# Dealing independent filler matmuls to the first steps and to the closing iterations of an attention loop, with two query loads moved ahead of it

## The chip, the cores and the metric

One Trainium2 chip, one core of it. The metric is the device time of one execution, in microseconds (us). The kernel before took 986.68 us (median of three runs, 985.72 to 988.01).

## What is computed

One layer of a hybrid encoder, on 1024 prompt rows and 64 sample rows of 1024 channels:

```python
h = rms_norm(x, norm_w) @ w_in          # 6144 columns: q, k, v, z of two branches, two gates
# branch sb: stick-breaking attention, 8 heads of 64
w = exp(log_beta + suffix_sum(log_keep))          # over all earlier keys
# branch cb: softmax attention over a band of chunks, with a relative bias, 8 heads of 64
p = softmax(q.k/8 + bias)
h = sigmoid(g_sb) * ((o_sb * silu(z_sb)) @ w_proj_sb) + sigmoid(g_cb) * ((o_cb * silu(z_cb)) @ w_proj_cb)
y = x + h @ w_out
```

The sample rows attend to 512 cached keys as well. Keys and values are outputs too.

## The kernel before, in words

Everything lies in one function whose Python code writes out the order of every engine's instructions. Each engine works through its own list in that order and waits on semaphores. TensorE multiplies float32 values as three products of rounded parts (`hi*hi`, `hi*lo`, `lo*hi`).

Stages: the input projection (to about 524 us), a lead (524 to 548), the attention loop (548 to 831), a tail (831 to 848), the projection of branch cb (L974) and the output projection (L1488).

**The attention loop** runs over a list `seq` of 136 steps: branch sb, then cb; in each four pairs of heads; in each pair t = 8 (the sample rows, one step for both heads), then t = 0 to 7, two heads each. A step passes through a pipeline over the iterations i of the loop:
- `qk(i)`: the scores, TensorE L1080 into `z`. In sb a sigmoid on ScalarE follows (L1083), in cb a VectorE operation with the bias (L1085).
- in sb `mid` one iteration later: a VectorE scan (L1102) on `be`. In cb `soft` (ScalarE exp, L1093) and then `mid` (VectorE reciprocal L1104, ScalarE scaling L1105).
- `tr(i - 3)`: transposes on TensorE (L1133) into `pt`, which has two PSUM buffers; ScalarE (L1142, L1138) or VectorE (L1144) copies them to `wT`.
- `av` at the next iteration, when two steps of a pair of row blocks are there: TensorE L1172 into `o`; VectorE multiplies it with the gate `zt` (L1181 in sb, L1183 in cb); GpSimd issues the store of `zt` (L745).

At t = 8 or 0 and others `prefetch` issues loads for later steps from the SyncE queue (SP): queries `sq` through `load_q` (four transfers by the helper at L51), keys `ks`, values (L785 to L787), and `zt` (L1150).

**The fill.** A generator `run_fill` holds matmuls that do not depend on the attention. `fill(n)` writes out the next n of them. They are:
- four units of 72 matmuls (L832), each in three pieces of 24 for columns 0 to 383, 384 to 767 and 768 to 1087. Piece 1 of a unit starts with the split of the next weights: ScalarE rounds `wraw` to `whi` (L116), VectorE or GpSimd makes the rest `wlo` (L123). A piece ends with a ScalarE evacuation to `sg` (L807).
- then the projection of branch sb, `proj_sb`: 24 groups of 12 matmuls (L932) on the accumulator `acc`, which has two PSUM buffers. Two groups share a gate tile `gt` (L912, two buffers). VectorE evacuates each group (L936). Of every six groups the last two have 320 columns, the others 384.

The lead takes 6 x 24 = 144 of the matmuls and issues the loads of the first pair between them. The loop deals the third unit (72) over branch sb, in proportion to the width of a step, and 252 plus 12 over branch cb. The fourth unit is held back until the loop's iteration 73: before that `fill` only notes what it owes, and iteration 73 pays it at once:

```python
if prog[0] == len(units) - 2 and "sb" not in late:
    owed[0] = n
    return
```

Four iterations behind the last step (i = 136 to 139) drain the pipeline, with no fill. In the tail, `load_og` loads branch cb's outputs by column piece (L889, into `ot`, two buffers for two pairs of heads each), `make_og` rounds them on ScalarE (L893) and subtracts on GpSimd (even pairs) and VectorE (odd pairs, L898); the order is fill(46), make_og(0), fill(24), make_og(1), the rest of the fill, make_og(2). L974 needs piece 0.

Of the kernel before, what the change touches and what calls it, by code (L numbers as in the profile page):

```python
# [32 lines left out]
def hybrid_step_kernel(ctx: ExitStack, tc: tile.TileContext, x_prompt, x_sample, c_sbk, c_sbv, c_cbk, c_cbv,  # L33
# [512 lines left out]
    with ExitStack() as ph:  # L546
# [104 lines left out]
        for i in range(len(pairs)):  # L651
            bank, s1, u2, u3 = {}, {}, {}, {}
            for s in range(7):
                n = 7 * i + s
# [135 lines left out]
    def load_q(b, p, ci):  # L790
        x, y = CH[ci] if ci < 3 else (NP, T)
        if ci < 3:
            y = min(y, NP)
        place_q(alloc_q((b, p), ci), d_qT[b][p][:], x, y)
# [393 lines left out]
    def prefetch(b, p, t):  # L1188

        nb_, np_ = (b, p + 1) if p + 1 < NPAIR else ("cb", 0) if b == "sb" else (None, None)  # L1190
        if t == 8:
            load_q(b, p, 1)
        elif t == 0:
            load_q(b, p, 2)
        if nb_ is None:
            return
        if t == 2:
            load_k(nb_, np_, 0)
        elif t == 3:
            load_k(nb_, np_, 1)  # L1200
        elif t == 5:
            load_q(nb_, np_, 3)
        elif t == 6:
            load_q(nb_, np_, 0)
        elif t == 7:
            load_v(nb_, np_)
        if b == "cb" and t == 4:
            load_bias(2 * np_)
            load_bias(2 * np_ + 1)
# [15 lines left out]
    load_vl()  # L1225
    load_k("sb", 0, 1)
    for f in (lambda: load_q("sb", 0, 3), lambda: load_k("sb", 0, 0), lambda: load_q("sb", 0, 0),
              lambda: (load_v("sb", 0), load_z("sb", 0, 4)), lambda: None, lambda: None):
        fill(24)
        flush()  # L1230
        f()
    make_vl()
    FP = 180
    n_sb = 72
    n_cb = 72 * (len(units) - 2) - n_sb + FP
    wt = {"sb": lambda n: n, "cb": lambda n: n + 150}
    tot = {b: sum(wt[b](band(b, t)[1]) for bb, p, t, hd in seq if bb == b) for b in ("sb", "cb")}
    amount = {"sb": n_sb, "cb": n_cb}
    acc, emitted = 0.0, 0
    LAG = 3  # L1240
    avq = []
    for i in range(len(seq) + LAG + 1):
        m = 0
        if i < len(seq):
            b, p, t, hd = seq[i]
            if b == "cb" and p == 0 and t == 8 and hd == 0:
                sbx.close()
                yst = ExitStack()
                late["y"] = yst.enter_context(tc.tile_pool(name="ay", bufs=2))
            if (b, p, t, hd) == ("sb", 3, 6, 0):  # L1250
                load_bias(0)
                load_bias(1)
        if 0 < i <= len(seq) and seq[i - 1][0] == "cb":
            soft(i - 1)
        if 1 < i <= len(seq) + 1 and seq[i - 2][0] == "cb":
            mid(i - 2)
        if i < len(seq):
            qk(i)
            if hd == 0:
                if t % 2 == 1 or t == 8 and (b, p) != ("sb", 0):  # L1260
                    load_z(b, p, t // 2 if t < 8 else 4)
                prefetch(b, p, t)
            acc += amount[b] * wt[b](band(b, t)[1]) / tot[b]
            if (b, p, t) == ("cb", 0, 8):
                acc += 12
            m = int(acc) - emitted
            emitted += m
        if 0 < i <= len(seq) and seq[i - 1][0] == "sb":
            mid(i - 1)
        flush()  # L1270
        if i == len(seq) // 2 + LAG + 2:
            late["sb"] = True
        fill(m // 2)
        while avq:
            av(*avq.pop(0))
        if 0 <= i - LAG < len(seq):
            tr(i - LAG)
            b, p, t, hd = seq[i - LAG]
            if t == 8 or hd == 1 and t % 2 == 1:
                avq.append((b, p, t // 2 if t < 8 else 4))  # L1280
        fill(m - m // 2)
# [73 lines left out]
    for ci in range(3):  # L1355
        if ci < 2:
            load_og("cb", ci, late["y"])
        fill((46, 24, 100000)[ci])
        if ci == 2:
            load_gcb(0)  # L1360
            load_og("cb", ci, late["y"])
# [212 lines left out]
```

## Time and profile before

| | us |
|---|---|
| median of three runs | 986.68 |
| lowest, highest | 985.72, 988.01 |
| the profiled execution | 985.0 |
| its span, first to last instruction | 983.2 |
| TensorE matmul busy in the span | 957.4 |
| VectorE, ScalarE, GpSimd busy | 594.5, 479.3, 394.1 |

The profiled execution's time is 1.8 us more than its span. The granted TensorE clock is 1.000 over the span. A row of a time line has the start, the length, the engine and line, the operation, what it writes and reads, and how many instructions were merged (x); in brackets stands how long the engine was idle before it and what ended that. PE is TensorE, DVE VectorE, ACT ScalarE, POOL GpSimd, SPq the SyncE queue.

### The profile page before, as it was taken

What the parts mean: (1) busy time and instruction counts of PE and PEld (TensorE: products, weight loads), DVE (VectorE), ACT (ScalarE), POOL (GpSimd) and SP (SyncE); (2) the same over time, 40 slices, a digit from 0 to 9 for tenths busy, and PEclk for the clock granted to TensorE, in tenths of its full rate; (3) what the DMA queues carried; (4) which work ended last, traced back from release to release, by engine and by line L of the source; (5) the groups of instructions that cost most, each with busy time, mean ns of one, the idle gap of its engine ahead of it and who ended that gap; (6) DMA issues with size and microseconds to landing.
All of it is one profiled execution on the core that took longest, in us unless ns stands there. A gap on an engine that the chain in (4) does not pass through costs nothing.

```text
span 983.2 us, 20553 instructions
## 1 busy us (share of the span) xinstructions
PE 957.4 (97%) x7620; PEld 913.0 (93%) x7620; DVE 594.5 (60%) x1168; ACT 479.3 (49%) x1056; POOL 394.1 (40%) x389
## 2 busy tenths in 40 slices
PE   5999999999999999999999899998999999999998
PEld 5999999999999999999999788887888887999998
DVE  5456664796454655533322479776677765689745
ACT  6544443344443433433332567666886875466320
POOL 3276664115444576556523100111421101486551
PEclk9999999999999999999999999999999999999999
DMA  6727567533656565565424999667798862762642
GB/s 230 229 89 239 193 234 255 161 98 120 183 178 199 157 184 169 151 196 173 128 73 127 263 225 250 175 185 184 212 269 238 227 177 84 236 201 74 219 131 76
DMA packets 176585, 176.82 MB, mean 180 GB/s; under 512 B 33825, under 2 KB 160669, under 8 KB 176358
## 3 DMA queue, kind: packets, MB, share of 16 engines
q1 hardware_dynamic: 164950, 160.50, 55.7%
q10 hardware_dynamic: 8720, 8.33, 2.6%
q0 software_dynamic: 2816, 6.69, 2.0%
q8 instruction: 60, 0.98, 0.5%
q14 instruction: 39, 0.32, 0.1%
HBM read 113.46 MB, written 62.00 MB: 178 GB/s over the span
## 4 chain that ended last, share of the span: by engine, by line
PE 89%; ACT 3%; DMA 2%; SPq 2%; DVE 2%; issue 1%; POOL 1%; DVEq 0%; ACTq 0%; POOLq 0%
PE b L672 30%; PE acc L466 19%; PE b L1488 8%; PE o L1172 7%; PE pt L1133 6%; PE z L1080 6%; PE b L974 5%; PE acc L932 4%; PE acc L832 2%; SPq L51 1%; ACT wT L1142 1%; DMA wrawx<-in_w_in_dram 1%; PE pk L351 1%; DMA ks<-d_ksbT 1%; PE pt L279 1%
## 5 line engine op out<-in xcount | busy, mean ns | idle before, releaser
L1133 PE MATMUL pt<-ident,be 128*128 128x128 f32 (+1 forms) x568 | 87.5, 278 | 6.2 <-DVE sm L1085 1.8
L1080 PE MATMUL z<-ks,sq 128*128 128x320 f32 (+5 forms) x384 | 84.9, 330 | 1.8 <-DMA sq<-d_qsbT 1.5
L1102 DVE TENSOR_TENSOR_SCAN be<-be,imp 128x128 f32<-128x128 f32 (+7 forms) x64 | 83.4, 1341 | 5.2 <-ACT be L1083 5.1
L1133 PEld LDWEIGHTS pt<-ident,be 128*128 128x128 f32 (+1 forms) x568 | 65.2, 140 | 18.8 <-issue 5.7
L1142 ACT ACTIVATE wT<-pt 128x512 f32<-128x512 f32 (+3 forms) x125 | 57.1, 485 | 49.3 <-PE pt L1133 48.0
L466 PE MATMUL acc<-whi,xa 128*128 128x256 f32 x256 | 74.2, 292 | 0.0
L466 PE MATMUL acc<-wlox,xm 128*128 128x256 f32 x256 | 70.7, 278 | 0.0
L466 PE MATMUL acc<-whi,xm 128*128 128x256 f32 x256 | 70.7, 278 | 0.0
L466 PE MATMUL acc<-wlo,xa 128*128 128x256 f32 x256 | 70.7, 278 | 0.0
L466 PE MATMUL acc<-whix,xb 128*128 128x256 f32 x256 | 70.6, 278 | 0.0
L466 PE MATMUL acc<-whix,xm 128*128 128x256 f32 x256 | 70.6, 278 | 0.0
L680 DVE TENSOR_TENSOR u<-b,s 128x256 f32<-128x256 f32 (+1 forms) x56 | 24.2, 440 | 73.4 <-PE b L672 71.9
L1080 PEld LDWEIGHTS z<-ks,sq 128*128 128x128 f32 x384 | 64.8, 189 | 3.5 <-DMA sq<-d_qsbT 1.2
L1172 PE MATMUL o<-wT,vp 128*64 128x256 f32 (+1 forms) x608 | 66.6, 357 | 0.1
L1172 PEld LDWEIGHTS o<-wT,vp 128*64 128x64 f32 x608 | 43.9, 136 | 22.9 <-issue 5.5
L123 POOL TENSOR_TENSOR wlo<-wraw,whi 128x1024 fp32r<-128x1024 f32 x15 | 36.6, 2437 | 51.6 <-ACT whi L116 46.4
L745 POOL DMA_DIRECT2D d_osb<-zt x20 | 10.8, 542 | 114.3 <-DVE zt L1181 102.9
L1105 ACT ACTIVATE be<-be,sm 128x640 f32<-128x640 f32 (+5 forms) x68 | 47.2, 694 | 9.7 <-DVE sm L1104 9.5
L436 POOL TENSOR_TENSOR whix<-ws,whix 128x512 fp32r<-128x512 f32 x28 | 37.1, 1324 | 32.5 <-ACT whix L435 32.5
L1083 ACT ACTIVATE be<-z 128x384 f32<-128x384 f32 (+6 forms) x104 | 47.2, 492 | 3.9 <-PE z L1080 3.4
L1093 ACT ACTIVATE be<-be,sm 128x640 f32<-128x640 f32 (+5 forms) x68 | 47.2, 695 | 3.5 <-DVE sm L1085 3.0
L466 PEld LDWEIGHTS acc<-whi,xa 128*128 128x128 f32 x256 | 47.9, 188 | 0.1
(306 smaller groups left out, 3196.3 us busy)
## 6 DMA issues: line engine op xcount, KB each, us to landing
wraw<-in_w_in_dram SPq DMA_DIRECT2D x31, 512.0 KB, 4.4
wrawx<-in_w_in_dram SPq DMA_DIRECT2D x17, 512.0 KB, 4.3
sq<-d_qsbT SPq DMA_DIRECT2D x32, 192.0 KB, 6.2
sq<-d_qcbT SPq DMA_DIRECT2D x32, 192.0 KB, 5.4
xt<-in_x_prompt_dram SPq DMA_DIRECT2D x8, 512.0 KB, 5.8
d_kcbT<-hl SPq DMA_DIRECT2D x8, 512.0 KB, 4.4
d_qcbT<-hl SPq DMA_DIRECT2D x8, 512.0 KB, 3.1
d_ksbT<-hl SPq DMA_DIRECT2D x16, 256.0 KB, 2.7
```

The lines of the kernel that those rows point to most:

```text
L466: TE.matmul(ps, x, w, start=m == 0, stop=m == len(steps) - 1)
L672: TE.matmul(ps[:, :m], w[:, hl_, k], right[s](x)[:, k, a:b], start=s < 3 and k == 0 and e == 0, stop=k == 3 and e == 2, skip_group_check=s ...
L974: TE.matmul(pp[uu][:, :n], w[:, p, uu * 128:uu * 128 + 128], g[:, a:e], start=p == 0 and m == 0, stop=p == NPAIR - 1 and m == 2)
L1080: TE.matmul(z[:, :m], s[:, e, q0:q0 + 128], ks[:, h, o + x:o + y], start=e == parts[0][0], stop=e == parts[-1][0])
L1083: A.activation(be[:r, x:y], z[:r, :m], AF.Sigmoid, scale=-0.125)
L1093: A.activation(be[:, :n], be[:, :n], AF.Exp, bias=kp[:, j:j + 1], scale=-1.0, accum_out=kp[:, 2:3])
L1102: V.tensor_tensor_scan(be[:r, n - 1::-1], be[:r, n - 1::-1], im[:, ::-1], 0.0, op0=OP.mult, op1=OP.max)
L1105: A.activation(be[:r, :n], be[:r, :n], AF.Copy, scale=kp[:r, 3:4])
L1133: TE.transpose(pt[:kr, x, :r], be[:r, kb * 128:kb * 128 + kr], ident[:r, :r])
L1142: A.activation(w[:, sl:sl + m, q0:q0 + r], pt[:, :m, :r], AF.Copy)
L1172: TE.matmul(o[hd * 64:hd * 64 + 64, c0:c1], vv[:kr, kb, hd * 64:hd * 64 + 64], wT[b, p, j, hd, s // 4][:kr, s % 4, c0:c1] if j < 4 else wT ...
L1488: TE.matmul(ps[:, t], left[s](xs_, k)[:, ts_], wt_[:, k], start=s < 3 and t == k == e == 0, stop=k == 3 and e == 2, skip_group_check=s > 2 ...
```

## The change

```diff
-        if t == 8:
-            load_q(b, p, 1)
-        elif t == 0:
-            load_q(b, p, 2)
+        if t in (8, 0) and (b, p) != ("sb", 0):
+            load_q(b, p, 1 if t == 8 else 2)
...
     for f in (lambda: load_q("sb", 0, 3), lambda: load_k("sb", 0, 0), lambda: load_q("sb", 0, 0),
-              lambda: (load_v("sb", 0), load_z("sb", 0, 4)), lambda: None, lambda: None):
+              lambda: (load_v("sb", 0), load_z("sb", 0, 4)), lambda: load_q("sb", 0, 1), lambda: load_q("sb", 0, 2)):
...
-    amount = {"sb": n_sb, "cb": n_cb}
+    early = {("sb", 0, 8, 0): 12, ("sb", 0, 0, 0): 8, ("sb", 0, 0, 1): 8,
+             ("cb", 0, 8, 0): 18, ("cb", 0, 0, 0): 8, ("cb", 0, 0, 1): 8}
+    amount = {b: n - sum(m for e, m in early.items() if e[0] == b) for b, n in (("sb", n_sb), ("cb", n_cb))}
...
-            if (b, p, t) == ("cb", 0, 8):
-                acc += 12
+            acc += early.get((b, p, t, hd), 0)
             m = int(acc) - emitted
             emitted += m
+        else:
+            m = 8
...
-        fill((46, 24, 100000)[ci])
+        fill((22, 24, 100000)[ci])
```

In sb 28 of the 72 fill matmuls go to the first three steps. In cb 34 are meant for the first three, and 218 are dealt evenly, where 252 and an extra 12 were. The four closing iterations get 8 each, half ahead of the transposes and half behind them. The first fill of the tail shrinks from 46 to 22. What is written out between the loop's last `av` and L974 falls from 97 matmuls to 81.

**TensorE at the start of sb.** Before, one fill matmul (L832) stands among the scores of the first four steps, ahead of the first transposes:

```order
L1080 MATMUL z<-kss,sqs 128x288 x8
L832 MATMUL acc<-xa,whi 128x384
L1080 MATMUL z<-ks,sq_7310 128x128 x4
L1080 MATMUL z<-ks,sq_7310 128x256 x2
L1133 MATMUL pt<-ident,be 128x128 x4
L1133 MATMUL pt<-ident,be 64x128
```

Now 12, 8 and 8 follow the first three steps; here the last of the three, up to the same transposes:

```order
L1080 MATMUL z<-ks,sq_7310 128x128 x2
L832 MATMUL acc<-xm,wlo 128x384
L832 MATMUL acc<-xm,whi 128x384
L832 MATMUL acc<-xb,whi 128x384
L832 MATMUL acc<-xm,wlo 128x384
L832 MATMUL acc<-xa,whi 128x384
L832 MATMUL acc<-xm,whi 128x384
L832 MATMUL acc<-xa,wlo 128x384
L832 MATMUL acc<-xa,whi 128x384
L1080 MATMUL z<-ks,sq_7310 128x256 x2
L1133 MATMUL pt<-ident,be 128x128 x4
L1133 MATMUL pt<-ident,be 64x128
```

So 28 matmuls stand ahead of the first transposes, where one did. Up to the first scores that need the second query tile (128x512), 30 stand where three did, and up to those of the second head 30 where four did.

**ScalarE at the same place.** The 24th of those matmuls ends a piece, and the 25th brings the split of the fourth unit's weights. In the difference of ScalarE's order (+ is new) the evacuation and the rounding come ahead of the fourth step's sigmoid and of the first copies to `wT`:

```order
 L1083 ACTIVATE be<-z 128x288 x2
 L1083 ACTIVATE be<-z 128x128 x2
+L807 ACTIVATE sg<-acc 128x384
+L116 ACTIVATE whi<-wraw 128x1024
 L1083 ACTIVATE be<-z 128x256
 L1142 ACTIVATE wT<-pt 128x4x128
```

They stood in the second pair of heads before. The subtraction of the same split (L123) moves on VectorE to a place between the second and third scan, and on SP a load of 512 KB for the next weights moves ahead of the second `zt` load; the two `load_q` keep their places on SP, directly behind the weights of the fourth unit.

**TensorE at the end of cb.** Before, from the last `av` but one, the three last steps' transposes come together:

```order
L1172 MATMUL o<-wT,vp 64x256 x8
L1172 MATMUL o<-wT,vp 64x128 x4
L1133 MATMUL pt<-ident,be 128x128 x5
L932 MATMUL acc<-xa,whi 128x384
L932 MATMUL acc<-xb,whi 128x384
L1133 MATMUL pt<-ident,be 128x128 x15
L1172 MATMUL o<-wT,vp 64x256 x8
L1172 MATMUL o<-wT,vp 64x128 x4
```

Now 6, 8 and 8 fill matmuls stand between these four groups of transposes, and 8 ahead of the last `av`; here the second of these stretches:

```order
L1133 MATMUL pt<-ident,be 128x128 x5
L932 MATMUL acc<-xa,whi 128x384
L932 MATMUL acc<-xb,whi 128x384
L932 MATMUL acc<-xa,wlo 128x384
L932 MATMUL acc<-xa,whi 128x384
L932 MATMUL acc<-xb,whi 128x384
L932 MATMUL acc<-xa,wlo 128x384
L932 MATMUL acc<-xa,whi 128x384
L932 MATMUL acc<-xb,whi 128x384
L1133 MATMUL pt<-ident,be 128x128 x5
```

So 30 stand in the drain where 2 did. At the start of cb the first five steps have no fill in either order: iteration 73 pays 45 matmuls at once now, and paid 25 before.

## Prediction

> **What bounds the kernel now.** The page first: TensorE is busy nearly throughout, so I looked for the time in which it is not.
>
> ```profile
> PE 957.4 (97%) x7620; PEld 913.0 (93%) x7620; DVE 594.5 (60%) x1168; ACT 479.3 (49%) x1056; POOL 394.1 (40%) x389
> ```
>
> The change adds and removes no matmul. A matmul moved from one busy place to another costs nothing; one moved into a gap is worth its length. So the time changes by the change in TensorE's idle time, and the view by windows says how much there is in the stages that the change touches: start, end, then busy time of PE, PEld, DVE, ACT, POOL, the clock, DMA share, GB/s.
>
> ```profile
> 548.00:676.00 128.00, 123.46 (x963) 102.93 (x963) 96.15 (x106) 85.88 (x207) 14.12 (x29) 1.00 0.87 222
> 676.00:721.00 45.00, 42.15 (x323) 36.59 (x321) 28.60 (x102) 35.45 (x80) 14.88 (x23) 1.00 0.67 195
> 721.00:823.00 102.00, 100.73 (x792) 87.88 (x793) 75.80 (x283) 78.39 (x177) 16.83 (x26) 1.00 0.78 211
> 823.00:831.00 8.00, 6.60 (x53) 4.54 (x50) 3.75 (x10) 2.30 (x5) 0.54 (x1) 1.00 0.05 18
> 831.00:848.00 17.00, 15.87 (x97) 15.29 (x97) 9.94 (x13) 4.76 (x9) 7.03 (x6) 1.00 0.55 162
> ```
>
> Idle: 4.54 in sb, 2.85 at the start of cb, 1.27 in the rest of cb, 1.40 in the drain, 1.13 in the tail: 11.2 us, the most that the change could touch. A fill matmul of 384 columns takes 0.174 us (24 in 4.17), one of 320 columns 0.147 (they start 0.15 apart):
>
> ```profile
> 524.04 4.17 PE acc L832 x24
> 831.00 0.31 PE L932 MATMUL acc<-xa,whi 128*128 128x320 f32 x1
> 831.15 0.31 PE L932 MATMUL acc<-xb,whi 128*128 128x320 f32 x1
> ```
>
> **Start of sb.** TensorE's own time line shows five waits; the length in brackets is the wait.
>
> ```profile
> 551.32 0.77 PE L1133 MATMUL pt<-ident,be 128*128 128x128 f32 x5 [0.95 <-DVE be L1102]
> 552.67 0.95 PE L1172 MATMUL o<-wT,vs 128*64 128x64 f32 x20 [0.17 <-ACT wT L1142]
> 556.08 0.71 PE L1080 MATMUL z<-ks,sq 128*128 128x512 f32 x2 [1.01 <-DMA sq<-d_qsbT]
> 557.68 0.70 PE L1080 MATMUL z<-ks,sq 128*128 128x512 f32 x2 [0.50 <-DMA sq<-d_qsbT]
> 563.17 0.63 PE L1133 MATMUL pt<-ident,be 128*128 128x128 f32 x4 [0.17 <-DVE be L1102]
> 546.78 0.94 SPq L110 DMA_DIRECT2D wraw<-in_w_in_dram  x1
> 547.76 7.50 SPq L51 DMA_DIRECT2D sq<-d_qsbT  x8
> wraw<-in_w_in_dram SPq DMA_DIRECT2D x1, 512.0 KB, 8.0
> sq<-d_qsbT SPq DMA_DIRECT2D x4, 128.0 KB, 5.7
> ```
>
> Moving the two `load_q` does nothing by itself. On SP they stood directly behind the weights of the fourth unit and still do, and SP issued them back to back from 547.76, so the queries land when they landed. What helps is that TensorE asks later: 26 more matmuls stand ahead of the scores at 557.68, 26 x 0.174 = 4.5 us, and without its 2.6 us of waits before that TensorE comes there at 557.7 + 4.5 - 2.6 = 559.6, after the queries. Both DMA waits go, and the first 0.95 too.
>
> What is late next is ScalarE. The rounding of the next weights now precedes a sigmoid and the copies to `wT`. The weights are there at 546.78 + 8.0 = 554.8, about when ScalarE comes to them (the 24th matmul ends at about 554.3); the rounding takes 1.05 us, and VectorE's subtraction, now between two short scans, 1.23:
>
> ```profile
> 837.26 1.05 ACT L116 ACTIVATE whi<-wraw 128x1024 fp32r<-128x1024 f32 x1
> 596.11 1.23 DVE L123 TENSOR_TENSOR wlo<-wraw,whi 128x1024 fp32r<-128x1024 f32 x1 [0.80 <-ACT whi L116]
> 561.28 0.61 DVE L1181 SCALAR_TENSOR_TENSOR zt<-o,vl,zt 128x128 f32<-128x128 f32 x2 [2.61 <-PE z L1080]
> ```
>
> Rounding to 555.9, a sigmoid of about 0.4 and copies of about 0.85 end ScalarE's work near 557.0 (an estimate from such lengths in the trace); TensorE is there at about 556.6, so `av` waits about 0.4. The next weights' load, now ahead of the `zt` load on SP, costs 512 KB at 222 GB/s, 2.4 us. VectorE already waited 2.61 there (the scores named had long been done; the gate was missing), but TensorE is about 2 us later itself, so I keep the wait of 0.17 that came of it; without that cover it would be about 1 us. From 2.8 to 0.5: **-2.3** (between -2.8 and -1.3).
>
> **Later in sb.** Fill per pair falls from 17 or 18 to 10 or 11. Three waits of 0.40 like the first row here have a fill matmul ahead of them now, and the split that caused the second row is gone: -0.75 at most.
>
> ```profile
> 587.07 0.95 PE L1172 MATMUL o<-wT,vs 128*64 128x64 f32 x20 [0.40 <-ACT wT L1142]
> 597.00 0.61 PE L1080 MATMUL z<-ks,sq 128*128 128x384 f32 x2 [0.25 <-ACT be L1083]
> ```
>
> Against that, each step has less cover for the scans (VectorE 96 of 128 us). I take **-0.5** (-0.75 to +0.5).
>
> **Start of cb.** The largest wait stands ahead of the burst that pays what was owed:
>
> ```profile
> 679.99 1.15 PE L1133 MATMUL pt<-ident,be 128*128 128x128 f32 x8 [1.78 <-DVE sm L1085]
> ```
>
> The matmuls meant for the first three steps of cb are owed too and come at the same iteration, 45 instead of 25. The wait stays: **0** (-0.4 to +0.4, for what ScalarE queues in the burst).
>
> **Rest of cb.** About 54 fill matmuls per pair instead of 63, that is 1.6 us less cover in 35. ScalarE is busy 78 of 102 us; the present 1.27 of idle may grow: **+0.3** (-0.2 to +1.3).
>
> **Drain.** Three waits between the transposes, 1.40, and the last `av` takes 2.88 where the one before takes 2.38:
>
> ```profile
> 820.92 2.38 PE L1172 MATMUL o<-wT,vp 128*64 128x256 f32 x24
> 824.76 0.73 PE L1133 MATMUL pt<-ident,be 128*128 128x128 f32 x5 [0.41 <-DVE wT L1144]
> 825.96 0.77 PE L1133 MATMUL pt<-ident,be 128*128 128x128 f32 x5 [0.47 <-ACT wT L1142]
> 827.25 0.74 PE L1133 MATMUL pt<-ident,be 128*128 128x128 f32 x5 [0.52 <-DVE wT L1144]
> 827.92 2.88 PE L1172 MATMUL o<-wT,vp 128*64 128x256 f32 x24
> ```
>
> Eight matmuls are 1.4 us, more than any of these: **-1.75** (to -1.0).
>
> **Tail.** Here cover is taken away. I count from the end of the last `av`, 830.80.
>
> ```profile
> 831.66 0.54 POOL L745 DMA_DIRECT2D d_ocb<-zt  x1 [6.94 <-DVE zt L1183]
> 835.59 1.77 ACT L893 ACTIVATE og<-ot 128x384 fp32r<-128x384 f32 x4 [7.18 <-DMA gt<-d_gsb]
> 836.20 1.99 POOL L898 TENSOR_TENSOR og<-ot,og 128x384 fp32r<-128x384 f32 x2 [4.00 <-ACT og L893]
> 838.39 2.47 POOL L123 TENSOR_TENSOR wlo<-wraw,whi 128x1024 fp32r<-128x1024 f32 x1 [0.20 <-ACT whi L116]
> 837.29 3.98 DVE L898 TENSOR_TENSOR og<-ot,og 128x384 fp32r<-128x384 f32 x2
> 841.20 1.01 DVE L936 TENSOR_TENSOR xm<-acc,gt 128x384 f32<-128x384 f32 x2
> 841.80 0.44 PE L932 MATMUL acc<-xa,whi 128*128 128x384 f32 x1 [0.83 <-DVE xm L936]
> 848.08 0.51 PE L974 MATMUL b<-og,whi 128*128 128x384 f32 x2
> ```
>
> The roundings begin at +4.8, when the last store has landed (issued at 831.66); that does not move against `av`. VectorE's subtractions follow, and every evacuation behind them waits. With two accumulators TensorE gets two groups of 12 past the last evacuation ahead of them. Before: 1 + 36 matmuls, then 24 more, to +10.2, and 0.83 of wait. Now 9 + 12 and 24 more, 9 of 320 columns and 36 of 384: 1.3 + 6.3 = +7.6. All 81 are 33 x 0.147 + 48 x 0.174 = 13.2 us.
>
> When are the subtractions done now? VectorE was busy with an evacuation until 837.29; now it is free earlier and starts when the second rounding is done, +5.8. Its two operations took 1.32 and 2.75, each ending 0.42 after the GpSimd operation that was running (838.19 and 840.86); where both engines began together, four took 2.3 us:
>
> ```profile
> L898 DVE TENSOR_TENSOR og<-ot,og x2: 1316/2031/2746, 837.3 to 838.5; 128x384 fp32r<-128x384 f32 x2
> 852.13 1.96 POOL L898 TENSOR_TENSOR og<-ot,og 128x320 fp32r<-128x320 f32 x2 [6.85 <-ACT og L893]
> 852.51 1.93 DVE L898 TENSOR_TENSOR og<-ot,og 128x320 fp32r<-128x320 f32 x2 [3.73 <-ACT og L893]
> ```
>
> Taking turns from +5.4, the four end near +8.2, ahead of the 2.47 us split. The evacuation (0.55) frees the accumulator at +8.8: a wait of 1.2. The next loads, roundings and subtractions move up with them; the last group starts at +13.2 and L974 at +15.0. Idle 15.0 - 13.2 = 1.8 for 1.13: **+0.7** (-1.1 with no wait; +2.3 with the present durations, below).
>
> The Trainium skill, "SBUF — State Buffer", section "Who interferes with whom", says that a VectorE instruction with two SBUF inputs contends with a GpSimd instruction that reads SBUF, and that the one issued first holds the shared ports for its whole length. The trace agrees by the 0.42 us. By that rule the split could still be issued first and hold the ports; the sum would then be 984.7 (the first rival) and with turns as at 852 it is 983.1.
>
> **Sum.** -2.3 - 0.5 + 0 + 0.3 - 1.75 + 0.7 = -3.55 us against the profiled execution's 985.0 (1.8 outside its span stay): 981.4. That execution was 1.7 below the median; on the median 986.68 - 3.55 = **983.1 us**, -0.36%. A measurement of this kernel can tell about 0.2% from no change, 2.0 us.
>
> **Rivals.**
> 1. The tail starves: VectorE gets no turn between GpSimd's operations, the subtractions take 3.98 again and only begin 0.65 earlier. Then L974 starts at +16.6, idle 3.4, the term is +2.3: 986.68 - 1.95 = 984.7. For it the row of 3.98; against it the rows at 852.
> 2. The start of sb gains nothing: ScalarE's split, the gate that lands 2.4 later and the delayed scans make as many waits as go. Sum -1.25: 985.4. For it the 2.61 at VectorE; against it that TensorE asks 2 us later.
> 3. Slower: the weights of the fourth unit. ScalarE takes instructions in order, so if they land late, sigmoid, copies and TensorE stand until then. They landed before the queries behind them; if they shared the queue with these and ended with the last one (issued 554.75, 5.7 to landing: 560.5), they would be 5.7 later: -3.55 + 5.7 = +2.15, 988.8. It decides from 3.6 us late. Against it: nothing ahead of them on SP changes. The Trainium skill, "DMA: Bandwidth & Descriptors", section "Queues, rings and completion order", adds that descriptors on one DMA engine are taken in ring order while completion is not first in, first out; the trace's order of landing agrees with the first half.
>
> That the cb half does not do what it says is no rival but counted: term 0.
>
> **Chances.** Forecast 0.66, first rival 0.18, second 0.08, third 0.08. The first sits on the edge of 0.2%, so I give 0.04 of it to faster: faster 0.70, same 0.22, slower 0.08. For the range I take the better ends of sb and the tail (-5.7: 981.0) and, upward, both first rivals nearly whole (986.2); the third is left out.
>
> **What would show it.** Right: no DMA wait on `sq` at the first 128x512 scores; no wait over 0.2 between the last transposes; the 1.78 still there; L974 about 15 us behind the last `av`, with VectorE's two subtractions under 3 us. Wrong: a wait of over 1 us for ScalarE in the first steps of sb, L974 at 16 or more behind `av`, or new waits for L1093 and L1105 in cb of over 1 us in all.

## The result, and the profile after

The changed kernel took **983.04 us** (median of six runs, 981.92 to 984.82) beside 986.88 us for the kernel before (six runs, 985.72 to 988.01): ratio 0.9963, 95% interval 0.9949 to 0.9977, so 3.8 us faster, by more than the 0.2% that counts as a difference here. The forecast was 983.1. The profiled execution took 981.92 us.

The page's first line, to be held against that of before:

```profile
PE 957.2 (98%) x7620; PEld 915.8 (93%) x7620; DVE 591.3 (60%) x1168; ACT 476.5 (49%) x1056; POOL 394.5 (40%) x389
```

TensorE's busy time is the same within 0.3 us; the span fell by 3.1. Of these 3.1 us, 0.8 lie ahead of the first scores of branch sb (548.05 before, 547.26 after), where both programs issue the same instructions; over all fourteen traces of this document that point lies between 547.26 and 549.62. To compare stages I cut both traces at the same events: first scores of sb, of its second pair, of cb, of cb's second pair; 10.1 us ahead of the last `av`'s end; that end; the first L974. Columns as before. First the kernel before, then the changed one:

```profile
548.05:577.25 29.20, 26.41 (x199) 21.54 (x198) 21.90 (x25) 18.64 (x46) 2.71 (x5) 1.00 0.96 238
577.25:674.46 97.21, 95.46 (x754) 79.83 (x753) 73.58 (x79) 66.28 (x160) 10.87 (x23) 1.00 0.84 216
674.46:717.30 42.84, 39.99 (x307) 34.46 (x305) 26.46 (x92) 33.51 (x76) 13.95 (x22) 1.00 0.66 186
717.30:820.70 103.40, 102.14 (x798) 90.04 (x797) 77.66 (x291) 79.30 (x178) 18.30 (x29) 1.00 0.80 219
820.70:830.80 10.10, 8.70 (x73) 5.85 (x71) 4.53 (x13) 4.25 (x9) 0.54 (x1) 1.00 0.05 15
830.80:848.08 17.28, 16.15 (x97) 15.57 (x98) 10.11 (x13) 4.76 (x9) 7.03 (x6) 1.00 0.55 160
```

```profile
547.26:578.12 30.86, 29.61 (x220) 25.33 (x219) 23.02 (x26) 19.29 (x48) 3.24 (x6) 1.00 0.91 233
578.12:671.42 93.30, 91.78 (x733) 75.60 (x732) 72.45 (x78) 63.66 (x158) 10.29 (x22) 1.00 0.86 220
671.42:718.22 46.80, 43.71 (x320) 38.26 (x319) 28.56 (x94) 34.45 (x79) 15.44 (x24) 0.96 0.63 184
718.22:819.96 101.74, 100.08 (x789) 88.81 (x790) 76.79 (x291) 79.01 (x178) 17.30 (x27) 1.00 0.80 211
819.96:830.06 10.10, 10.10 (x85) 8.92 (x81) 5.01 (x12) 2.81 (x6) 0.56 (x1) 1.00 0.30 93
830.06:845.02 14.96, 13.51 (x82) 13.24 (x82) 7.24 (x11) 4.80 (x9) 7.54 (x6) 1.00 0.62 185
```

Length less PE busy is idle time. Before: 2.79, 1.75, 2.85, 1.26, 1.40, 1.13; after: 1.25, 1.52, 3.09, 1.66, 0, 1.45. The third row also has a clock of 0.96: at the start of cb TensorE ran for 3.41 us at half speed, which the trace of the kernel before does not show (the rows are in the last section).

The start of sb. TensorE's time line has no wait for `sq` any more and two others, one for ScalarE and one for VectorE; VectorE's own row shows where it stood, at a gate product behind 2.08 us of idle time (the row names the scores; that it was the gate tile is shown by e5 below):

```profile
555.55 0.95 PE L1172 MATMUL o<-wT,vs 128*64 128x64 f32 x20 [0.45 <-ACT wT L1142]
564.56 0.63 PE L1133 MATMUL pt<-ident,be 128*128 128x128 f32 x4 [0.81 <-DVE be L1102]
562.67 0.61 DVE L1181 SCALAR_TENSOR_TENSOR zt<-o,vl,zt 128x128 f32<-128x128 f32 x2 [2.08 <-PE z L1080]
```

Branch cb. The 1.78 is where it was, and the low clock follows it; further on a wait named for ScalarE grew from 0.38 to 0.69, while VectorE sat in a subtraction of 384 columns for 2.10 us beside GpSimd's split:

```profile
676.94 1.26 PE L1133 MATMUL pt<-ident,be 128*128 128x128 f32 x8 [1.78 <-DVE sm L1085]
697.07 0.44 PE L1133 MATMUL pt<-ident,be 128*128 128x128 f32 x2 [0.69 <-ACT be L1105]
692.95 2.10 DVE L898 TENSOR_TENSOR xb<-ot,xa 128x384 fp32r<-128x384 f32 x1 [5.89 <-ACT xa L893]
692.23 2.40 POOL L123 TENSOR_TENSOR wlo<-wraw,whi 128x1024 fp32r<-128x1024 f32 x1 [5.18 <-issue]
```

Drain and tail. The transposes run without a wait, the last `av` takes 2.38 us instead of 2.88, and the tail has one wait, 1.45. VectorE shows where it comes from: its subtractions of the first column chunk (834.68) are done early, but those of the second (840.20, 842.07) stand in front of two evacuations:

```profile
825.86 0.71 PE L1133 MATMUL pt<-ident,be 128*128 128x128 f32 x5
827.68 2.38 PE L1172 MATMUL o<-wT,vp 128*64 128x256 f32 x24
843.15 0.41 PE L932 MATMUL acc<-xa,whi 128*128 128x320 f32 x1 [1.45 <-DVE xm L936]
845.02 0.51 PE L974 MATMUL b<-og,whi 128*128 128x384 f32 x2
834.68 2.35 DVE L898 TENSOR_TENSOR og<-ot,og 128x384 fp32r<-128x384 f32 x2 [0.41 <-ACT og L893]
840.20 0.96 DVE L898 TENSOR_TENSOR og<-ot,og 128x384 fp32r<-128x384 f32 x1 [1.74 <-ACT og L893]
842.07 0.56 DVE L898 TENSOR_TENSOR og<-ot,og 128x384 fp32r<-128x384 f32 x1 [0.91 <-ACT og L893]
842.55 0.95 DVE L936 TENSOR_TENSOR xm<-acc,gt 128x384 f32<-128x384 f32 x2
841.51 0.52 ACT L893 ACTIVATE og<-ot 128x384 fp32r<-128x384 f32 x1 [0.43 <-DMA ot<-d_ocb]
```

### The profile page after: what moved, and what is told of

It reads as the page before. It is cut to its first block, busy times and chain, and to the rows that moved or that the text cites. A ratio compares the mean times of both kernels' runs of the same rounds, so it can differ in the third digit from the quotient of the medians.

```text
span 980.1 us, 20557 instructions
## 1 busy us (share of the span) xinstructions
PE 957.2 (98%) x7620; PEld 915.8 (93%) x7620; DVE 591.3 (60%) x1168; ACT 476.5 (49%) x1056; POOL 394.5 (40%) x389
## 5 line engine op out<-in xcount | busy, mean ns | idle before, releaser
L1133 PE MATMUL pt<-ident,be 128*128 128x128 f32 (+1 forms) x568 | 87.5, 278 | 5.5 <-DVE sm L1085 1.8
L1133 PEld LDWEIGHTS pt<-ident,be 128*128 128x128 f32 (+1 forms) x568 | 65.3, 140 | 17.8 <-issue 5.0
L1172 PEld LDWEIGHTS o<-wT,vp 128*64 128x64 f32 x608 | 46.6, 138 | 22.0 <-issue 7.6
L123 POOL TENSOR_TENSOR wlo<-wraw,whi 128x1024 fp32r<-128x1024 f32 x15 | 36.3, 2423 | 53.8 <-ACT whi L116 48.6
L1105 ACT ACTIVATE be<-be,sm 128x640 f32<-128x640 f32 (+5 forms) x68 | 47.2, 694 | 10.8 <-DVE sm L1104 10.8
L466 PEld LDWEIGHTS acc<-whi,xm 128*128 128x128 f32 x256 | 48.0, 188 | 0.0
```

The source lines that it names most:

```text
L123: (eng or G).tensor_tensor(out=l, in0=raw, in1=h[:].bitcast(F32), op=OP.subtract)
L466: TE.matmul(ps, x, w, start=m == 0, stop=m == len(steps) - 1)
L1105: A.activation(be[:r, :n], be[:r, :n], AF.Copy, scale=kp[:r, 3:4])
L1133: TE.transpose(pt[:kr, x, :r], be[:r, kb * 128:kb * 128 + kr], ident[:r, :r])
L1172: TE.matmul(o[hd * 64:hd * 64 + 64, c0:c1], vv[:kr, kb, hd * 64:hd * 64 + 64], wT[b, p, j, hd, s // 4][:kr, s % 4, c0:c1] if j < 4 else wT ...
```

## The experiments

Ratios are to the kernel before, run on the same chip; below 1 is faster. They are the recorded ones and differ by up to 0.001 from the quotient of two medians (for e1 984.26 / 986.97 is 0.9973). 0.001 is about 1 us, and each interval spans about 1.2 to 1.6 us to either side, so a profile's waits settle more than a ratio does. Where two experiments are compared, it is by their ratios, and the interval of such a difference is wider still.

| run | ratio | 95% interval |
|---|---|---|
| changed kernel | 0.9963 | 0.9949 to 0.9977 |
| e1_sb_alone | 0.9967 | 0.9955 to 0.9979 |
| e2_end_alone | 0.9987 | 0.9976 to 0.9999 |
| e3_cb_alone | 1.0039 | 1.0024 to 1.0054 |
| e4_queries_early | 1.0015 | 1.0000 to 1.0030 |
| e5_gate_first | 0.9956 | 0.9942 to 0.9970 |
| e6_tail_gpsimd | 0.9961 | 0.9946 to 0.9976 |
| e7_release_early | 0.9952 | 0.9940 to 0.9964 |
| e8_three | 0.9928 | 0.9912 to 0.9943 |
| e9_subs_gpsimd | 1.0006 | 0.9992 to 1.0020 |
| e10_without_cb | 0.9975 | 0.9962 to 0.9987 |
| e11_all | 0.9970 | 0.9958 to 0.9982 |
| e12_gate_tail | 0.9955 | 0.9940 to 0.9969 |

**The parts alone.** First the sb half.

```diff
+    early = {("sb", 0, 8, 0): 12, ("sb", 0, 0, 0): 8, ("sb", 0, 0, 1): 8}
             if (b, p, t) == ("cb", 0, 8):
                 acc += 12
+            acc += early.get((b, p, t, hd), 0)
```

> The kernel before with the sb half of the change alone (12, 8 and 8 fill matmuls in the first three steps of sb). Theory (the time changes by TensorE's idle time, stage by stage): no DMA wait on sq, a wait of about 0.45 us for wT and one of about 0.8 us at the first transposes of step 128x512 as in the changed kernel's trace, idle time of sb from 4.5 to about 2.8 us; the drain, the tail and the 1.78 us wait of cb as before: 1.8 to 2.8 us faster than before. Rival (the gain of the whole change comes from the drain; in sb waits only change their place): 0 to 0.5 us faster.

Measured: 984.26 us against 986.97, ratio 0.9967, most of the gain: 2.7 us by the medians, 3.3 by the ratio. Idle time of sb in its profile is 1.14 + 1.52 = 2.66 us against 4.54, as expected, but not by the waits expected: the 0.8 is not there, and the wait for `wT` is 1.14 and not 0.45, since ScalarE's rounding stood for the fourth unit's weights, which landed late:

```profile
558.62 0.95 PE L1172 MATMUL o<-wT,vs 128*64 128x64 f32 x20 [1.14 <-ACT wT L1142]
556.75 1.06 ACT L116 ACTIVATE whi<-wraw 128x1024 fp32r<-128x1024 f32 x1 [0.60 <-DMA wraw<-in_w_in_dram]
```

So the third rival's mechanism exists, but it costs 0.7 us at this place (1.14 for 0.45), where the rival had the weights 5.7 us late. Of the ten profiles with the sb half of the change four have it (1.14 here, 1.15 in e8, 1.19 in e11, 1.74 in e9); the other six have 0.43 to 0.45. Moving the two `load_q` changes nothing by itself: with that edit alone every engine's list of instructions is the same as before.

Then the end alone.

```diff
         emitted += m
+    else:
+        m = 8
-    fill((46, 24, 100000)[ci])
+    fill((22, 24, 100000)[ci])
```

> The kernel before with the end of the change alone (8 fill matmuls in each of the four closing iterations, 22 instead of 46 ahead of the first og roundings). Theory: the three waits between the last transposes (1.40 us) and the 0.5 us by which the last av was longer go, the tail keeps one wait of about 1.4 us: 1.3 to 1.9 us faster than before, L974 about 15.0 us behind the last av. Rival (the tail starves, as the matmuls taken from it are missed there one for one): L974 16.5 us or more behind the last av, 0 to 0.5 us faster.

Measured: 0.9987. The three waits in the drain are gone, but the tail waits 2.61 us, and L974 comes 15.7 behind the last `av` with only 70 matmuls in between:

```profile
846.45 0.64 PE L932 MATMUL acc<-xa,whi 128*128 128x320 f32 x1 [2.61 <-DVE xm L936]
828.69 5.67 SPq L912 DMA_DIRECT2D gt<-d_gsb  x4
835.43 2.02 SPq L889 DMA_DIRECT2D ot<-d_ocb  x4
```

Without the cb half, 12 more matmuls are done in the attention, so the drain's 32 reach the point where the filler asks for its next gate and weights. SP stands in those gate loads for 5.67 us, and the `og` loads behind them are issued 0.4 us ahead of the last `av`'s end; in the changed kernel it is 3.2 us (826.86). The roundings begin 6.8 us behind `av` instead of 3.7. Their rows name the landing of the last `zt` store; first e2, then the changed kernel:

```profile
842.64 1.76 ACT L893 ACTIVATE og<-ot 128x384 fp32r<-128x384 f32 x4 [8.64 <-DMA d_ocb<-zt]
833.71 1.77 ACT L893 ACTIVATE og<-ot 128x384 fp32r<-128x384 f32 x4 [6.72 <-DMA d_ocb<-zt]
```

In both this store is issued 0.9 us behind `av`; it took 5.4 us to land in e2, with weights and `og` loads issued just ahead of it, and 2.0 in the changed kernel. So the tail starves, but for transfers, not for the ports; that the loads ahead of the store hold it up is argued from their order.

The cb half alone.

```diff
+    early = {("cb", 0, 8, 0): 18, ("cb", 0, 0, 0): 8, ("cb", 0, 0, 1): 8}
-            if (b, p, t) == ("cb", 0, 8):
-                acc += 12
+            acc += early.get((b, p, t, hd), 0)
```

> The kernel before with the cb half of the change alone (18, 8 and 8 in the first three steps of cb in place of 12). Theory: the matmuls are owed until the release, so the wait of 1.78 us stays and the burst behind it grows by about 20; new waits for ScalarE's normalisation of 0.3 to 0.6 us in all: 0 to 0.6 us slower. First rival (the fill reaches the first steps): the 1.78 is gone, 1.5 us faster or more. Second rival (the granted clock of 0.87 to 0.94 that the changed kernel's trace shows at 671 to 690 comes from this part): a clock below 0.95 there, 1.5 us slower or more.

Measured: 1.0039, 3.9 us slower, at a clock of 1.00: neither my theory nor a rival. The 1.78 stays, as I said. The rows of cb's start, of the rest of cb, of the drain and of the tail, at the same events:

```profile
674.77:720.47 45.70, 42.55 (x321) 37.22 (x320) 28.58 (x94) 34.45 (x79) 15.45 (x24) 1.00 0.64 186
720.47:820.63 100.16, 98.49 (x772) 86.84 (x771) 75.64 (x286) 77.06 (x174) 16.38 (x27) 1.00 0.80 215
820.63:830.74 10.11, 8.70 (x73) 6.52 (x71) 4.78 (x15) 4.87 (x10) 1.48 (x2) 1.00 0.24 83
830.74:851.25 20.51, 18.09 (x109) 17.76 (x110) 8.05 (x14) 5.17 (x10) 7.39 (x6) 1.00 0.49 152
847.62 0.41 PE L932 MATMUL acc<-xa,whi 128*128 128x320 f32 x1 [2.42 <-DVE xm L936]
```

Idle time in cb grew by 0.30 + 0.41, as the changed kernel's did; but the attention now does 12 matmuls fewer, they stand in the tail, and the tail waits 2.42 us instead of 1.13: 1.3 us that I had not looked for. That is 2.0 us of idle time, about half of the 3.9; another 0.6 at the start of sb (a wait of 0.95 behind the gate tile) lies where the two programs are alike. Which matmuls are left for the tail shifts every load that the filler issues there.

Whether the three parts are independent shows when the cb half is left out of the whole (the changed kernel, with cb as before):

```diff
-    early = {..., ("cb", 0, 8, 0): 18, ("cb", 0, 0, 0): 8, ("cb", 0, 0, 1): 8}
+            if (b, p, t) == ("cb", 0, 8):
+                acc += 12
```

> The changed kernel without its cb half (cb again with the 12 extra matmuls at its first step, nothing else early), so the sb half and the end together. Theory (terms add only where the tail keeps its cover: without the cb half 69 matmuls are left for the tail instead of 81, as in the run of the end alone): tail with a wait of about 2.6 us instead of 1.45, cb about 0.6 us less idle: within 0.8 us of the changed kernel. Rival (the parts add as they were measured alone, -0.33, -0.13 and +0.39%): 0.9 us or more faster than the changed kernel, 4.5 us faster than before.

Measured: 0.9975, 1.2 us behind the changed kernel where at most 0.8 was expected (the intervals overlap). The tail has 69 matmuls and one wait of 2.21, the gate loads again stand ahead of the `og` loads on SP for 5.68 us, and the last store takes 4.9 us to land. The rival, the sum of the parts (-0.33 - 0.13 = -0.46%), lies outside the interval of this run; since the parts have intervals of their own, the traces say it more clearly. Alone the cb half costs 3.9 us, within the whole it costs nothing and may help: with its 12 matmuls left for the tail, the `og` loads go out ahead of the second pair of gate loads (826.86 and 832.14).

**Landing earlier instead of asking later.** The kernel before, its fill untouched, with the queries ahead of the fourth unit's weights:

```diff
-  lambda: (load_v("sb", 0), load_z("sb", 0, 4)), lambda: None, lambda: None):
+  lambda: (load_v("sb", 0), load_z("sb", 0, 4), load_q("sb", 0, 1), load_q("sb", 0, 2)), lambda: None, lambda: None):
```

> The kernel before, with nothing of the fill changed, but with the first pair's later queries issued on SP ahead of the fourth unit's weights, 512 KB earlier in the queue. Theory (what the change did in sb was to let TensorE ask after the queries landed; earlier landing does the same for the two DMA waits): the queries land about 2.4 us earlier, the DMA waits of 1.01 and 0.50 us go, the 0.95 us wait for the first scan stays: 1.0 to 1.7 us faster. Rival (the scans or the gates that land later take the place of the waits on sq): 0 to 0.4 us faster, with waits for VectorE or ScalarE of over 1 us in 556 to 566.

Measured: 1.0015, no gain. Both DMA waits are gone, and one of 2.63 us is there instead, with a low clock behind it. VectorE waits 4.22 us for the first gate tile, and the scans behind it come late:

```profile
563.62 0.63 PE L1133 MATMUL pt<-ident,be 128*128 128x128 f32 x4 [2.63 <-DVE be L1102]
561.73 0.61 DVE L1181 SCALAR_TENSOR_TENSOR zt<-o,vl,zt 128x128 f32<-128x128 f32 x2 [4.22 <-DMA zt<-d_zsb]
```

The rival held in kind and was worse in size. The DMA engines are 0.95 busy in this stretch. The gate product starts 13.87 us behind the first scores of sb, where it was 13.23 before; so the gate was the next thing to be late all along, and it came 0.6 us later still. With the matmuls moved instead, TensorE has other work until then, and the gate costs it between nothing (e1) and 1.21 us (e6).

**The waits that are left.** The gate tile of sb ahead of the projection weights:

```diff
-  lambda: load_q("sb", 0, 1), lambda: load_q("sb", 0, 2)):
+  lambda: load_q("sb", 0, 1), lambda: (load_q("sb", 0, 2), load_z("sb", 0, 0))):
-  if t % 2 == 1 or t == 8 and (b, p) != ("sb", 0):
+  if (t % 2 == 1 or t == 8) and (b, p, t) not in (("sb", 0, 8), ("sb", 0, 1)):
```

> The changed kernel with the first gate tile of sb (zt of rows 0 to 255) loaded in the lead, ahead of the 512 KB of projection weights on SP instead of behind them. Theory (the 0.81 us wait at the first transposes of the second 128x512 step is VectorE standing behind a gate that lands late): that wait falls to 0.2 us or less, the rest of sb is unchanged: 0.5 to 0.8 us faster than the changed kernel, so 4.0 to 4.5 us faster than before. Rival (the wait comes from the scans themselves, which are in arrears since the split): the wait stays between 0.6 and 0.9 us, same time as the changed kernel.

Measured: 0.9956. The 0.81 is gone, VectorE goes through the gate products without idle time ahead of them, and the start of sb has 0.43 us of idle time. In size that is what was expected; the ratios of 0.9956 and 0.9963 alone would not show it.

```profile
560.73 0.58 DVE L1181 SCALAR_TENSOR_TENSOR zt<-o,vl,zt 128x128 f32<-128x128 f32 x2
```

The second chunk's subtractions in the tail, all on GpSimd:

```diff
-  (V if p % 2 else G).tensor_tensor(out=og(b, 1, p)[:, a:e], ...
+  (V if p % 2 and (b, ci) != ("cb", 1) else G).tensor_tensor(out=og(b, 1, p)[:, a:e], ...
```

> The changed kernel with all four og subtractions of the middle column chunk of cb on GpSimd, so that VectorE's two evacuations at 842.55 stand behind no subtraction. Theory (the one wait left in the tail, 1.45 us, is VectorE standing in its subtractions for roundings whose loads land late): the wait falls to 0.3 us or less, L974 comes 13.5 to 13.9 us behind the last av: 1.1 to 1.4 us faster than the changed kernel. Rival (the wait goes over to the next link: GpSimd's four subtractions end later than L974 needs them, or VectorE's evacuation waits for the accumulator's last matmul): L974 at 14.7 or later.

Measured: 0.9961, no gain by the ratio. In the profile the tail's idle time fell from 1.45 to 0.08 and L974 comes 13.6 behind `av`, as the theory said. But this execution had other waits in places where the two programs are alike, above all this one, which the changed kernel's trace lacks:

```profile
730.21 0.95 PE L1172 MATMUL o<-wT,vs 128*64 128x64 f32 x20 [1.43 <-DMA vs<-in_cache_cb_v_dram]
```

Its start of sb had 1.65 us of idle time instead of 1.25. That a saved 1.4 us did not show in the ratio is within its interval; that it was given back by such waits in general is not shown.

Gate and tail together (the diffs of e5 and e6):

> The changed kernel with the gate of sb loaded in the lead and the og subtractions of cb's middle chunk on GpSimd, the release left where it was. Theory (two waits in stages 280 us apart add): 0.8 + 1.4 = 2.2 us faster than the changed kernel, 5.5 to 6.5 us faster than before. Rival (what is taken out of sb comes back as a wait for a load, since the transfers are no faster): 1.4 us or less faster than the changed kernel.

Measured: 0.9955, no better than the gate alone, where 0.994 was expected. Sb kept its gain (0.43 idle), the tail 0.9 of its 1.4 (0.53 idle), but the profile has 2.44 idle in cb instead of 1.66, with a wait of 0.91 at 728, and the low clock again. By the ratio the rival is ahead; the interval does not decide.

The release of the last unit's matmuls at the first iteration of cb, so that the early matmuls are done where the table puts them:

```diff
-        if i == len(seq) // 2 + LAG + 2:
+        if i == len(seq) // 2:
             late["sb"] = True
+        if i == len(seq) // 2 + LAG + 2:
+            load_og("sb", 0, late["y"])
...
-        if ogq and now:
+        for _ in range(2 if len(ogq) > 8 else 1):
+            if ogq and now and "tbp" in late:
```

(The lines left out are the pool and the gate load, moved along with `load_og` out of the filler. Two roundings or subtractions of `og` are made per call until the arrears are gone. In this kernel, in e8 and in e11 the lines from L833 on have numbers lower by 4: L1129 is L1133, L1101 L1105, L894 L898, L889 L893.)

> The changed kernel with the hold on the last unit lifted five iterations earlier, at the first iteration of cb, and the loads of sb's og kept at the place where they were; so the 34 early matmuls of cb are done in its first three steps instead of owed. Theory: the wait of 1.78 us and the 0.44 us behind it go, and the low granted clock that followed it in the changed kernel's trace goes with it; the burst of 45 shrinks, so the 0.69 us wait for ScalarE falls below 0.3: 2.0 to 2.8 us faster than the changed kernel, 1.3 more in runs where the clock had been low. Rival (what sets the start of cb is VectorE and ScalarE, not TensorE: the matmuls are done earlier but the chain of steps ends when it did): 0 to 0.5 us faster, with waits of 1.5 us or more for DVE or ACT left in 671 to 690.

Measured: 0.9952. The 1.78, the 0.44 and the low clock are gone; but the 0.69 became 1.63 and the 0.49 at 722 became 0.85, so idle time in cb fell only from 4.75 to 4.33 us. Between theory and rival, then. The wait is named for ScalarE, which waited for VectorE, which sat 2.64 us in one subtraction beside two of GpSimd's:

```profile
697.70 0.55 PE L1129 MATMUL pt<-ident,be 128*128 128x128 f32 x3 [1.63 <-ACT be L1101]
697.03 0.61 ACT L1101 ACTIVATE be<-be,sm 128x384 f32<-128x384 f32 x1 [1.71 <-DVE sm L1100]
694.23 2.64 DVE L894 TENSOR_TENSOR xb<-ot,xa 128x384 fp32r<-128x384 f32 x1 [0.95 <-ACT xa L889]
694.46 1.99 POOL L894 TENSOR_TENSOR xb<-ot,xa 128x384 fp32r<-128x384 f32 x2
```

So I took these subtractions off VectorE, first without the early release (sb's and the second chunk of cb's, all on GpSimd):

```diff
-  (V if p % 2 else G).tensor_tensor(out=og(b, 1, p)[:, a:e], ...
+  (V if p % 2 and b == "cb" and ci != 1 else G).tensor_tensor(out=og(b, 1, p)[:, a:e], ...
```

> The changed kernel with all og subtractions of sb, and those of the middle column chunk of cb, on GpSimd. Theory (the waits named for ScalarE's normalisation at 697.07 and 722.38, 0.69 and 0.49 us, are VectorE's: its subtraction of 384 columns took 2.10 us beside a GpSimd instruction and 0.56 alone, and the reciprocals stand behind it): VectorE has no subtraction of over 1 us left between 690 and 760, both waits fall to 0.3 us or less, the wait of 1.45 us in the tail is gone: 2.0 to 2.6 us faster than the changed kernel, 0.6 to 1.0 of it in cb. Rival (ScalarE's queue, which rounds og in a burst there, sets these waits): they stay as they are, 1.1 to 1.4 us faster, from the tail alone.

Measured: 1.0006, the whole gain lost. The 0.69 and the 0.49 are gone, so they were VectorE's, but a wait for the queries of the next pair came in, and one of 1.42 for ScalarE (716.51), which stood at a rounding:

```profile
725.57 0.41 PE L1080 MATMUL z<-ks,sq 128*128 128x128 f32 x2 [2.13 <-DMA sq<-d_qcbT]
715.61 0.47 ACT L893 ACTIVATE xa<-ot 128x320 fp32r<-128x320 f32 x1 [1.66 <-DMA ot<-d_osb]
```

GpSimd's subtractions end later, so the four `ot` buffers come free later; SP, which loads them in order, issues the queries behind them at 717.78 (712.34 in the changed kernel), and ScalarE's roundings stand in front of its normalisations until the tiles land. Then with the early release and the gate (the diffs of e5, e7 and e9):

> The changed kernel with the gate of sb loaded in the lead, the hold on the last unit lifted at the first iteration of cb, and the og subtractions of sb and of cb's middle chunk on GpSimd. Theory (the four waits are independent, and the 1.63 and 0.85 us that came in with the early release are VectorE's subtraction held up beside GpSimd): 0.8 us from sb, 1.4 from the tail, 1.8 to 3.0 from cb: 4.0 to 5.2 us faster than the changed kernel, 7.5 to 9 us faster than before. Rival (with the release early ScalarE is short at 690 to 700, since it makes two og roundings per call there): waits for ScalarE of 1.5 us or more stay in cb, 2.5 to 3.2 us faster than the changed kernel.

Measured: 0.9970, 0.7 us behind the changed kernel where even the rival had 2.5 to 3.2 ahead of it. The form is the rival's, a wait of 2.38 for ScalarE, but not its reason: ScalarE was not short, it stood 2.27 us at a rounding whose tile had not landed (and the low clock followed):

```profile
701.53 0.93 PE L1129 MATMUL pt<-ident,be 128*128 128x128 f32 x4 [2.38 <-ACT be L1101]
699.54 0.52 ACT L889 ACTIVATE xa<-ot 128x384 fp32r<-128x384 f32 x1 [2.27 <-DMA ot<-d_osb]
```

Last, gate, early release and the tail's second chunk, with sb's subtractions left on both engines (the diffs of e5, e6 and e7):

> The changed kernel with three edits that lie in different stages: the gate of sb loaded in the lead, the hold on the last unit lifted at the first iteration of cb with the og subtractions of sb left on both engines, and the og subtractions of cb's middle chunk on GpSimd. Theory (idle time adds over stages): sb 0.8 us less idle than the changed kernel, cb 0.4 less as in the run with the early release alone (the waits of 1.63 and 0.85 us stay), tail 0.9 to 1.4 less: 2.1 to 2.6 us faster than the changed kernel, 5.8 to 6.6 us faster than before, and no low granted clock at the start of cb. Rival (time won in one stage comes back as a wait for a load in the next, as 0.5 to 1.4 us did in cb when gate and tail were changed together or the tail alone): 1.2 us or less faster than the changed kernel.

Measured: 979.13 us against 985.99, ratio 0.9928 (0.9912 to 0.9943): about 3.5 us ahead of the changed kernel, more than the 2.1 to 2.6 expected, and the best version here. Idle time at the start and in the rest of cb is 1.97 and 2.36 as expected, at a clock of 1.00, and none is left in the tail. The 0.8 of sb did not come in this execution: the gate's wait is gone, but the fourth unit's weights landed late.

```profile
556.85 0.95 PE L1168 MATMUL o<-wT,vs 128*64 128x64 f32 x20 [1.15 <-ACT wT L1138]
671.71:715.91 44.20, 42.23 (x320) 37.48 (x319) 27.93 (x93) 34.24 (x78) 14.87 (x24) 1.00 0.73 210
828.92:842.23 13.31, 13.31 (x82) 13.29 (x82) 5.92 (x9) 4.79 (x9) 9.45 (x8) 1.00 0.77 227
```

Between the same events this trace is 3.4 us shorter than that of the changed kernel: start of sb -0.3, start of cb -2.6, rest of cb +1.2, tail -1.6. Of the -2.6 at the start of cb, 1.1 is idle time and the rest busy time, most of it the low clock of that one trace of the changed kernel. So part of the surplus over the expectation is the clock.

## Why the prediction was right, and where not

| term | predicted | measured in the traces |
|---|---|---|
| start of sb | -2.3 | 1.25 - 2.79 = -1.5 |
| later in sb | -0.5 | 1.52 - 1.75 = -0.2 |
| start of cb | 0 | 3.09 - 2.85 = +0.2, and 1.1 of low clock |
| rest of cb | +0.3 | 1.66 - 1.26 = +0.4 |
| drain | -1.75 | 0 - 1.40 - 0.50 in the last `av` = -1.9 |
| tail | +0.7 | 1.45 - 1.13 = +0.3 |

The six terms make -2.7 for -3.55. Between the first scores of sb and L974 the two traces are 300.03 and 297.76 us long, 2.3 less. With a full clock it would be 3.4 less: e5 has the same program at the start of cb and a clock of 1.00 there, and the same 320 matmuls keep TensorE busy for 42.58 us where the changed kernel's trace has 43.71. The 0.7 us between 3.4 and 2.7 lies inside records that count as busy, as the 0.50 in `av` did; where is not shown.

So that the median came out within 0.1 us of 983.1 is in part luck. The two terms of sb gave 1.0 less than forecast and cb took 0.3 more; the drain and the tail gave 0.5 more, 0.7 stood in no term, and the low clock, in no term either, is there in some executions and not in others. A slip in the working: the better ends of sb and the tail take 2.3 off -3.55, to -5.85 and not -5.7, so the range would have begun at 980.8; nothing hangs on it.

- **Start of sb**: the DMA waits and the 0.95 went because TensorE asked later, and 0.45 came for 0.4, as worked out. What failed is "I keep the wait of 0.17": it became 0.81. The cover did not hold, and "about 1 us without it" was the right price. e5 shows the cause: the gate stood behind 512 KB of weights. Of the signs of being wrong, "a wait of over 1 us for ScalarE in the first steps of sb" did not show in this trace, but it did in four other executions with the same sb half (1.14 to 1.74); that the weights are there in time, with ScalarE coming to them at about the same moment, was a near thing.
- **Start of cb**: owed until the release, 1.78 unchanged: right. The low clock behind that wait was in none of the cases; e7, which removes the wait, has none there.
- **Rest of cb**: size right. ScalarE was named for it; e9 shows that VectorE's subtraction beside GpSimd stood behind it.
- **Drain**: right, mechanism and size.
- **Tail**: L974 at +14.96 for +15.0, though by another way. Of the 1.8 of idle time worked out, the wait of 1.2 did not come, since the roundings began at +3.7 and not at +4.8. They do wait for the last store, but "that does not move against `av`" failed: issued at +0.9 both times, the store landed after 2.0 us instead of 3.2; in the kernel before SP issues gate loads (831.79) right beside it, which in the changed kernel stand elsewhere (826.02 and 832.14). What was left of the 1.8, 0.6, became 1.45, since the second chunk's subtractions waited for their loads ahead of the evacuations. VectorE's two took 2.35 us, taking turns, so the first rival failed in the tail. Its mechanism, VectorE getting no turn between GpSimd's instructions, showed at the start of cb instead (e7).
- **"That the cb half does not do what it says ... term 0"**: right for the whole, and wrong as a part of its own: e3 and e10 show that it decides, by 12 matmuls, which loads stand ahead of `og`'s on SP.

## What to carry to other kernels

Where the DMA engines are nearly full (0.96 of the time here), giving the engine that waits something else to do was worth about 3 us (e1), and moving the transfer nothing (e4), because the next transfer, the gate, was as late. Moving a load ahead did pay where it passed one whose delay showed in no wait (e5). And look at several traces of one program before trusting the waits of one: the start of sb had 1.25 us of idle time in the changed kernel's trace and up to 2.1 in those of other runs with the same program there. Filler that issues loads is not neutral: when a table moves it, follow every load that it issues past the others on the same queue, since parts that gain alone may not add, and a part that loses alone may be needed. And the wait that a profile names may belong to an engine two steps back; follow the row of the named engine before moving its work.

## What the runs showed of the hardware

**A wait can cost more than its length, and where it falls decides.** Behind some waits of TensorE its granted clock was 0.50, ten times in these fourteen traces (leaving out the last microseconds of the program), for 3.41 us each time. The wait of 1.78 at the start of cb is in eleven of them; behind it the clock was low in five (the changed kernel, e2, e6, e10, e12) and full in six. Elsewhere a low clock followed waits of 2.61, 2.63, 2.38 and 2.21 (e2, e4, e11, e10), and in e2 two in a row of 1.18 and 0.47. It did not follow the 2.42 of e3, the 2.13 and the 1.74 of e9, or the 1.63 of e7 and e8.

The clock's records show what makes the difference. The three low stretches of e2 begin at 559.59, 682.47 and 846.31, that is 36 and 48 times 3.413 us apart, the two of e10 48 times; counted from the first record of the clock, all ten begin at a whole number of steps of 3.413 us. So time is divided into windows of that length, and the wait itself does not start one. Here are the window that holds the wait of 1.78 and the next one, first in the changed kernel, then in e5, whose program is the same there:

```profile
674.42:677.84 3.42, 1.64 (x16) 1.44 (x15) 1.75 (x7) 3.41 (x8) 0.31 (x1) 1.00 0.86 243
677.84:681.25 3.41, 3.41 (x18) 2.23 (x18) 0.55 (x3) 2.22 (x6) 0.00 (x0) 0.50 0.03 9
674.86:678.27 3.41, 2.07 (x14) 1.42 (x16) 1.04 (x7) 3.41 (x9) 0.00 (x0) 1.00 0.64 180
678.27:681.68 3.41, 3.41 (x31) 2.22 (x32) 0.03 (x1) 0.99 (x4) 0.00 (x0) 1.00 0.02 5
```

In the first the wait (675.16 to 676.94) lies within one window, which is busy for 0.48 of its length, and the next one is granted half the clock. In e5 the wait (674.36 to 676.14) is cut by a border, its window is busy for 0.61, and the clock stays full. Of the ten windows ahead of a low one nine are busy for 0.23 to 0.48 and one for 0.52; of all the others up to 965 us none is below 0.49 (0.495 in e3, 0.50 in e9). So in these traces a window that TensorE spends about half idle costs the next one half its clock. The waits of one window count together, and one and the same wait can lower the clock in one execution and not in the next. At the start of cb the low clock made TensorE's busy time longer by 0.9 to 1.5 us (1.1, 1.5 and 1.4 in the changed kernel, e6 and e12 against e5; 0.9 in e2 and e10 against e1). At about 1.2 us in five of eleven executions the 1.78 is worth about 2.3 us, an estimate. The Trainium skill, "TensorE: Matmul & The Clock Gate", section "Part 1: The HAM clock gate (the "warmup" mystery)", gives two states, full and half, and the half one after an idle window of about 3.4 us that runs freely. The 0.50, the windows of 3.41 us and that no wait restarts them agree; but the window need not be idle throughout, about half was enough here.

**GpSimd can hold VectorE.** A subtraction of 384 columns took VectorE 0.56 us alone (842.07), 2.10 beside GpSimd's split and 2.64 beside two of GpSimd's subtractions in e7, each time ending 0.42 behind GpSimd's. In e7 VectorE got no turn between GpSimd's two (1.02 us each); in the tail of the changed kernel (834.68) it did, and GpSimd's second took 1.32. What decides which is not shown. The Trainium skill, "SBUF — State Buffer", section "Who interferes with whom", has the instruction that was issued first hold the ports for its whole length. The row of 2.10 agrees, GpSimd's split being 0.72 us ahead; the row of 2.64 does not, since by its record VectorE began 0.23 us ahead of GpSimd's first.
